# Key and value compression of a sparse-attention layer: block rows stationary, W1's rounded halves moving, a constant matrix that folds

## The chip, the cores and the metric

The kernel runs on one core of a Trainium2 chip. The metric is the device time of one execution in microseconds (us); the kernel before has a median of 1343.45 us over three runs (1343.28 to 1351.97). The engines are TensorE (PE; PEld is its weight load), VectorE (DVE), ScalarE (ACT), GpSimd (POOL) and SyncE (SP), whose queue issues most loads.

## The reference, cut to what matters

The program is two decoder layers over 512 tokens of width 1024. Each has a mixer (sparse attention, gated linear attention, spatial gating) and a gated feed-forward part. The change touches one step of the sparse attention, the compression of raw keys and raw values into 31 block rows for each of two groups:

```python
def compress_blocks(k_raw, pos_emb, w1, w2):
    B, S, G, hd = k_raw.shape                    # 1, 512, 2, 64
    nc = (S - CMP_LEN) // CMP_STRIDE + 1         # 31 blocks of 32 tokens, 16 apart
    idx = np.arange(nc)[:, None] * CMP_STRIDE + np.arange(CMP_LEN)[None, :]
    blk = k_raw[:, idx] + pos_emb[None, None, :, None, :]
    blk = blk.transpose(0, 1, 3, 2, 4).reshape(B, nc, G, CMP_LEN * hd)
    return jax.nn.gelu(blk @ w1) @ w2            # w1: 2048 x 256, w2: 256 x 64
```

It is called for keys (then rotated) and for values, in each layer. A block of 32 tokens is two runs of 16, and each run belongs to two blocks, as the first half of one and the second half of another.

## The kernel before, in words

Everything is float32 at the input. Large products are made from three f32r products: an operand is split into a rounded half (ScalarE, `nc.scalar.copy` to f32r) and the rest (VectorE, a subtraction), here called hi and lo. `w_rows` (lines 278 to 284) loads a 512 KB piece of a weight into a `raw` buffer (three of them) with a SyncE issue, and `w_split` (lines 266 to 276) splits it into an `hl` buffer (four of them). `mm3` (lines 285 to 288) issues hi x hi, hi x lo and lo x hi. The scheduler orders each engine's instructions when the program is built; each engine then runs its list in order, waiting on semaphores.

The stretch of the mixer that matters runs so. The projection for the spatial gating (`uv`) ends. `proj_feat` (lines 477 to 487) projects raw keys and raw values, features on partitions: two PSUM banks of 128 x 512, one for keys and one for values, with their matmuls taken in turn. `ev_kv` (lines 542 to 550) takes each bank out in four VectorE products with `rb`, the row of inverse norms, into `kvS`, 128 x 8 x 66: partitions are (token parity, feature), then a pair number within a run of 16 tokens, then the runs of both groups and two columns of the position embedding (`pos_t`).

Beside this `uv` is normalised: squares on ScalarE (line 560), a short chain on VectorE (lines 561 to 564), four scalings on VectorE (567), four additions on GpSimd (568). Then TensorE makes the four spatial products (571), VectorE gates them (574), and the result is transposed (444) and split.

The compression follows, first keys, then values (lines 580 to 647): W1 comes in eight 256 KB loads into buffers of its own (`w1` and `qr` tags), unsplit. It is the stationary operand, 128 x 128 at a time, and 65 columns of `kvS` move, all in f32; 16 steps of 128 rows times two halves of 256 hidden features, accumulated into one PSUM tile (line 593). The position columns give a bias (597), a Gelu follows (601), then W2. The keys' result is rotated, transposed and split (612 to 625), the values' is copied four times and split (632 to 645).

After that come the gates projection (`c1`, 296 columns, whose weights are three more `hl` units) and the `gqk` feature projection.

Of the kernel before, what the change touches and what calls it, by code (L numbers as in the profile page):

```python
# [19 lines left out]
P = 128  # L20
# [42 lines left out]
def shape_constants():  # L63
# [46 lines left out]
    for h in range(GH):  # L110
        hb[h * DK : (h + 1) * DK, h] = 1
        hones[h * DK : (h + 1) * DK, h] = 1
    triu = (j[:, None] <= i[None, :]).astype(np.float32)
    cf = np.concatenate([rope, ropec, hb.reshape(P, -1), triu, hones,
                         np.ones((P, 1), np.float32)], axis=1).astype(np.float32)
# [8 lines left out]
def trunk_kernel(ctx: ExitStack, tc: tile.TileContext, a, out):  # L124
# [10 lines left out]
    def nm(s):  # L135
        uid[0] += 1
        return f"{s}_{uid[0]}"
# [26 lines left out]
    hones = cf[:, o : o + GH]  # L164
    o += GH
    ones1 = cf[:, o : o + 1]
    mb = cp.tile([P, 2 * P + NT * 32], BF16, name="mb")
    identb = mb[:, 0:P]
    dmask = mb[:, P : 2 * P]
# [278 lines left out]
    def mixer(l, norm, xkt, eu=None):  # L448
# [8 lines left out]
        def xs(k, s):  # L457
            return xkt[k // 2][:, k % 2, s, :]
# [15 lines left out]
                with tc.high_priority(offset=EP.get(wsite[0], EPRI)):  # L474
                    evac(t, ps)

        def proj_feat(c0, evac):

            us = [w_rows(w_in, k0 * P, 4, c0, 256) for k0 in (0, 4)]
            ps = [psum("g") for _ in range(2)]  # L480
            for k in range(KT):
                for b in range(2):
                    u = us[k // 4][:, :, k % 4, b * P : (b + 1) * P]
                    mm3(ps[b], u[:, 0], u[:, 1], xs(k, 0), xs(k, 1), k == 0, k == KT - 1)
            for b in range(2):
                with tc.high_priority(offset=EP.get(wsite[0], EPRI)):
                    evac(b, ps[b])

        def units(c0, w, nks):
            us, k0 = [], 0  # L490
# [5 lines left out]
        with tc.tile_pool(name=f"mx{l}", bufs=1, reuse_waits="tile") as mp:  # L496
# [13 lines left out]
            with tc.tile_pool(name=f"ma{l}", bufs=1, reuse_waits="tile") as ap:  # L510
# [24 lines left out]
                nc.scalar.dma_start(lngb[:, 1, :], a["sg_ln_b"][l : l + 1, :].to_broadcast([P, 256]))  # L535
                rb = norm.broadcast()


                kvS = [ap.tile([P, 8, 66], F32, name=nm("kvS")) for _ in range(2)]
                for w_i in range(2):  # L540
                    nc.gpsimd.tensor_copy(kvS[w_i][:, :, 64:66], pos_t(w_i, l).rearrange("p (s a) -> p a s", s=2))

                def ev_kv(b, ps):
                    for g in range(G):
                        gs = slice(g * 64, (g + 1) * 64)
                        src = ps[gs, :].rearrange("p (c a r) -> p r a c", a=8, r=2)
                        rbv = rb[gs, :].rearrange("p (c a r) -> p r a c", a=8, r=2)
                        for lp in range(2):
                            nc.vector.tensor_tensor(kvS[b][lp * 64 : (lp + 1) * 64, :, g * 32 : (g + 1) * 32],
                                                    src[:, lp], rbv[:, lp], op=ALU.mult)  # L550
                site("kc")
                proj_feat(C_KC, ev_kv)

                vmean = small(NT, "vmean", 1)
                nc.vector.tensor_scalar(vmean, vsum, 1.0 / 256, None, op0=ALU.mult)
# [24 lines left out]
                hts = []  # L580
                for w_i, nmw in enumerate("kv"):
                    w1 = a["cmp_w1_" + nmw][l]
                    ps = psum("o")[:, 0:130]
                    for u in range(8):
                        if u % 5 < 3:
                            wu = ap.tile([P, 2, 256], F32, tag="w1", name=nm("w1"), bufs=6)
                        else:
                            wu = mp.tile([P, 2, 256], F32, tag="qr", name=nm("w1"), bufs=4)
                        nc.sync.dma_start(wu, w1[u * 256 : (u + 1) * 256, :].rearrange("(k p) c -> p k c", p=P))
# [6 lines left out]
                    hb = small(2, "hb", 2)  # L596
                    nc.scalar.copy(hb, ps.rearrange("p (k c) -> p k c", k=2)[:, :, 64])
                    hid = tmp(124)
                    hT = hid.rearrange("p (k c) -> p k c", k=2)
                    for hh in range(2):  # L600
                        nc.scalar.activation(hT[:, hh].rearrange("p (g c) -> p g c", g=G),
                                             ps[:, hh * 65 : hh * 65 + 64].rearrange("p (g c) -> p g c", g=G)[:, :, 0:NC_],
                                             AF.Gelu_apprx_tanh, bias=hb[:, hh : hh + 1])
# [811 lines left out]
```

## Time and profile before

| what | value |
|---|---|
| median of three runs | 1343.45 us |
| profiled execution | 1343.64 us, span 1341.9 us |
| TensorE busy | 1298.7 us, 97% |
| VectorE, ScalarE, GpSimd busy | 949.1, 624.5 and 176.4 us |
| chain that ended last, by engine | PE 77%, DVE 12%, ACT 4% |

Busy time is the union of an engine's instructions. Matmuls overlap, so a mean of a matmul is longer than the distance to the next start. Idle time stands in brackets behind a row, with what ended it.

### The profile page before, as it was taken

The page shows a single profiled execution, that of the slowest core. Times are in us where ns is not written, and L with a number is a line of the kernel's source. Part 1 is how long each engine was busy: PE and PEld are TensorE (multiplying, and loading weights), DVE is VectorE, ACT ScalarE, POOL GpSimd, SP SyncE. Part 2 cuts the span into 40 slices and gives each one's busy share as a digit, 9 for nine tenths or more (in the row PEclk, how much of TensorE's full clock was granted, in tenths as well). Part 3 has the DMA queues.
Part 4 walks back from the last instruction along what each step waited for, and adds up shares of the span by engine and source line. Part 5 has one row for each costly group of instructions (what it writes and reads, how often), then busy time and mean ns, then how long its engine had stood idle before and what let it go on. Part 6 is the DMA issues. An engine that isn't in the chain of part 4 may idle for free.

```text
span 1341.9 us, 17478 instructions
## 1 busy us (share of the span) xinstructions
PE 1298.7 (97%) x6434; PEld 1054.7 (79%) x6434; DVE 949.1 (71%) x1661; ACT 624.5 (47%) x1164; POOL 176.4 (13%) x158
## 2 busy tenths in 40 slices
PE   6999999999999999999999999999999999999997
PEld 5888776777888888888888877767788888888785
DVE  5636889997865785586644498999778457736775
ACT  6344336665542543254442632667544435514532
POOL 2111021114000100010312102111220001000103
PEclk9999999999999999999999999999999999999999
DMA  8521131006335785384363302201343348754721
GB/s 280 156 81 48 32 95 32 17 17 159 109 99 121 206 213 152 105 203 111 96 181 97 91 21 63 79 17 33 91 129 95 110 120 205 225 126 126 195 88 64
DMA packets 128554, 150.41 MB, mean 112 GB/s; under 512 B 9034, under 2 KB 82516, under 8 KB 128468
## 3 DMA queue, kind: packets, MB, share of 16 engines
q1 hardware_dynamic: 115504, 128.31, 31.5%
q0 software_dynamic: 8704, 16.78, 7.4%
q10 hardware_dynamic: 4260, 4.20, 1.1%
q8 instruction: 51, 0.84, 0.3%
q14 instruction: 35, 0.29, 0.1%
HBM read 147.17 MB, written 2.10 MB: 111 GB/s over the span
## 4 chain that ended last, share of the span: by engine, by line
PE 77%; DVE 12%; ACT 4%; DMA 3%; issue 3%; POOL 1%; SPq 0%; ACTq 0%; DVEq 0%; POOLq 0%
PE psg L286 10%; PE psg L287 10%; PE psg L288 10%; PE pss L286 4%; PE pst L286 4%; PE pss L288 4%; PE pss L287 4%; PE pst L288 4%; PE pst L287 4%; PE pso L593 2%; DVE hl L274 2%; PE pst L1010 2%; PE pso L288 2%; PE pso L286 2%; PE pso L287 2%
## 5 line engine op out<-in xcount | busy, mean ns | idle before, releaser
L271 ACT CAST hl<-raw 128x1024 fp32r<-128x1024 f32 (+3 forms) x170 | 175.6, 1034 | 224.3 <-PE pst L288 66.2
L274 DVE TENSOR_TENSOR hl<-raw,hl 128x1024 fp32r<-128x1024 f32 (+3 forms) x170 | 207.8, 1223 | 100.3 <-ACT hl L271 97.5
L286 PE MATMUL psg<-hl,kt 128*128 128x512 f32 (+2 forms) x480 | 179.4, 375 | 4.1 <-ACT hl L271 2.1
L288 PE MATMUL psg<-hl,kt 128*128 128x512 f32 (+2 forms) x480 | 178.2, 372 | 0.0
L287 PE MATMUL psg<-hl,kt 128*128 128x512 f32 (+2 forms) x480 | 177.3, 370 | 0.0
L286 PEld LDWEIGHTS psg<-hl,kt 128*128 128x128 f32 x480 | 91.1, 190 | 19.0 <-DVE gqk L698 2.7
L288 PEld LDWEIGHTS psg<-hl,kt 128*128 128x128 f32 x480 | 91.1, 190 | 12.9
L287 PEld LDWEIGHTS psg<-hl,kt 128*128 128x128 f32 x480 | 91.0, 189 | 12.8
L287 PE MATMUL psg<-kt,hl 128*128 128x512 f32 x248 | 99.6, 402 | 1.2 <-DVE kt L249 1.2
L286 PE MATMUL psg<-kt,hl 128*128 128x512 f32 x248 | 99.6, 403 | 0.0
L288 PE MATMUL psg<-kt,hl 128*128 128x512 f32 x248 | 98.3, 398 | 0.0
L271 ACT CAST hl<-wx 128x1024 fp32r<-128x1024 f32 x48 | 50.3, 1049 | 78.6 <-PE pst L288 63.3
L274 DVE TENSOR_TENSOR hl<-wx,hl 128x1024 fp32r<-128x1024 f32 x48 | 58.7, 1223 | 18.0 <-ACT hl L271 17.4
L253 ACT CAST PT<-pst 128x384 fp32r<-128x384 f32 (+1 forms) x96 | 46.7, 519 | 37.9 <-PE pst L1010 37.6
L254 DVE TENSOR_TENSOR PT<-pst,PT 128x384 fp32r<-128x384 f32 (+1 forms) x96 | 54.8, 595 | 10.5 <-ACT PT L253 9.6
L1002 POOL TENSOR_TENSOR P<-P,rr 128x512 f32<-128x512 f32 x32 | 35.5, 1109 | 174.8 <-DVE rr L999 134.3
L1010 PE MATMUL pst<-ident,P 128*128 128x128 f32 x320 | 53.2, 277 | 2.6 <-DVE P L1004 2.6
L287 PEld LDWEIGHTS psg<-kt,hl 128*128 128x128 f32 x248 | 46.9, 189 | 9.9 <-DVE kt L249 2.0
L288 PEld LDWEIGHTS psg<-kt,hl 128*128 128x128 f32 x248 | 46.8, 189 | 8.0
L286 PEld LDWEIGHTS psg<-kt,hl 128*128 128x128 f32 x248 | 46.7, 189 | 7.8 <-ACT kt L253 0.3
L286 PE MATMUL pss<-hl,kt 128*128 128x512 f32 x128 | 50.3, 393 | 1.7 <-DVE ft L1302 1.3
L288 PE MATMUL pss<-hl,kt 128*128 128x512 f32 x128 | 50.0, 390 | 0.0
(442 smaller groups left out, 3139.6 us busy)
## 6 DMA issues: line engine op xcount, KB each, us to landing
raw<-in_w_gate_dram SPq DMA_DIRECT2D x44, 512.0 KB, 3.8
raw<-in_w_up_dram SPq DMA_DIRECT2D x44, 512.0 KB, 4.4
raw<-in_w_in_dram SPq DMA_DIRECT2D x32, 512.0 KB, 3.7
raw<-in_w_down_dram SPq DMA_DIRECT2D x20, 512.0 KB, 3.9
raw<-in_w_down_dram SPq DMA_DIRECT2D x36, 256.0 KB, 4.1
raw<-in_w_out_dram SPq DMA_DIRECT2D x16, 512.0 KB, 4.0
w<-in_cmp_w_k_dram SPq DMA_DIRECT2D x16, 256.0 KB, 5.4
w<-in_cmp_w_v_dram SPq DMA_DIRECT2D x16, 256.0 KB, 3.1
```

The lines of the kernel that those rows point to most:

```text
L253: nc.scalar.copy(hi, src)
L254: nc.vector.tensor_tensor(lo, src, hi.bitcast(F32), op=ALU.subtract)
L271: nc.scalar.copy(hl[:, 0, 0:n], raw[:, 0:n])
L274: e_.tensor_tensor(hl[:, 1, 0:n], raw[:, 0:n], hl[:, 0, 0:n].bitcast(F32), op=ALU.subtract)
L286: nc.tensor.matmul(ps, lh, rh, start=start, stop=False, skip_group_check=skip)
L287: nc.tensor.matmul(ps, lh, rl, start=False, stop=False, skip_group_check=skip)
L288: nc.tensor.matmul(ps, ll, rh, start=False, stop=stop, skip_group_check=skip)
L593: nc.tensor.matmul(ps[:, hh * 65 : (hh + 1) * 65], wu[:, kk, hh * P : (hh + 1) * P], kvS[w_i][:, s % 8, s // 8 : s // 8 + 65], start=s == ...
L1002: nc.gpsimd.tensor_tensor(ps_[i], ps_[i], rr[:, i : i + 1].to_broadcast([P, P * (i + 1)]), op=ALU.mult)
L1010: nc.tensor.transpose(T[:, c : c + P], ps_[i][:, j * P : (j + 1) * P], ident)
```

## The change

Four things change in the mixer of each layer, and one constant is added.

First, `proj_feat` gets an argument `apart`: all 24 matmuls of the keys run before the 24 of the values, and the keys are taken out as soon as theirs are done. Second, the eviction copies PSUM to `kvS` on ScalarE (four copies each for keys and values), multiplies by `rbk` (a rearranged copy of `rb`) in one VectorE operation, and splits the result into `kvR`, in which hi and lo of a column lie side by side. The two position columns move to the ends of the 66 columns. Third, W1 is loaded by `w_rows` in four 512 KB pieces and split like other weights. The stationary operand is now 64 columns of `kvR` with both halves, 128 columns; W1's hi and lo move, 256 columns each. The first eight steps and the last eight accumulate in two halves of one PSUM tile. Fourth, the sums over hi and lo, over the two runs of a block and over the position row are made by a constant matrix `fold` (128 x 2 x 62, part of the constants' load): the PSUM tile is copied to SBUF, and four f32 matmuls per operand multiply it by `fold`. The Gelu then needs no bias.

The core of the diff:

```diff
+    fold = np.zeros((2, 64, 2 * NC_), np.float32)
+    r31 = np.arange(NC_)
+    fold[0, 0, :] = 1
+    fold[0, 1 + r31, r31] = 1
+    fold[0, 33 + r31, NC_ + r31] = 1
+    fold[1, r31, r31] = 1
+    fold[1, 32 + r31, NC_ + r31] = 1
+    fold[1, 63, :] = 1
+    fold = np.repeat(fold, 2, axis=1).transpose(1, 0, 2)
...
-        def proj_feat(c0, evac):
+        def proj_feat(c0, evac, apart=False):
...
+            for bs in ((0,), (1,)) if apart else ((0, 1),):
+                for k in range(KT):
+                    for b in bs:
+                        u = us[k // 4][:, :, k % 4, b * P : (b + 1) * P]
+                        mm3(ps[b], u[:, 0], u[:, 1], xs(k, 0), xs(k, 1), k == 0, k == KT - 1)
+                for b in bs:
+                    with tc.high_priority(offset=EP.get(wsite[0], EPRI)):
+                        evac(b, ps[b])
...
+                rbk = ap.tile([P, 8, 32], F32, name=nm("rbk"))
+                for lp in range(2):
+                    hs = slice(64 * lp, 64 * lp + 64)
+                    nc.scalar.copy(rbk[hs], rb[hs, :].rearrange("p (c a r) -> p r a c", a=8, r=2)[:, lp])
...
+                kvR = [ap.tile([P, 8, 66, 2], F32R, name=nm("kvR")) for _ in range(2)]
...
                         for lp in range(2):
-                            nc.vector.tensor_tensor(kvS[b][lp * 64 : (lp + 1) * 64, :, g * 32 : (g + 1) * 32],
-                                                    src[:, lp], rbv[:, lp], op=ALU.mult)
+                            nc.scalar.copy(kvS[b][lp * 64 : (lp + 1) * 64, :, 1 + g * 32 : 33 + g * 32], src[:, lp])
+                    k4 = kvS[b][:, :, 1:65].rearrange("p a (g c) -> p a g c", g=G)
+                    nc.vector.tensor_tensor(k4, k4, rbk.unsqueeze(2).to_broadcast([P, 8, G, 32]), op=ALU.mult)
+                    split_psum(kvR[b][:, :, :, 0], kvR[b][:, :, :, 1], kvS[b])
                 site("kc")
-                proj_feat(C_KC, ev_kv)
+                proj_feat(C_KC, ev_kv, True)
...
-                    ps = psum("o")[:, 0:130]
-                    for u in range(8):
...
-                        for kk in range(2):
-                            s = u * 2 + kk
-                            for hh in range(2):
-                                nc.tensor.matmul(ps[:, hh * 65 : (hh + 1) * 65], wu[:, kk, hh * P : (hh + 1) * P],
-                                                 kvS[w_i][:, s % 8, s // 8 : s // 8 + 65],
-                                                 start=s == 0 and hh == 0, stop=s == 15 and hh == 1, skip_group_check=True)
...
+                    ps = psum("o")
+                    for u in range(4):
+                        wu = w_rows(a["cmp_w1_" + nmw][l], u * 512, 4, 0, 256)
+                        for kk in range(4):
+                            s = u * 4 + kk
+                            s8 = s // 8
+                            for half in range(2):
+                                nc.tensor.matmul(ps[:, s8 * 256 : (s8 + 1) * 256], kvR[w_i][:, s % 8, 2 * s8 : 2 * s8 + 64, :].rearrange("p c h -> p (c h)"),
+                                                 wu[:, half, kk, :], start=s % 8 == 0 and half == 0, stop=s % 8 == 7 and half == 1,
+                                                 skip_group_check=True)
+                    hs_ = tmp()
+                    nc.scalar.copy(hs_, ps)
+                    hps = psum("s")
+                    for kk in range(2):
+                        for s8 in range(2):
+                            nc.tensor.matmul(hps[:, kk * 62 : kk * 62 + 62], hs_[:, s8 * 256 + kk * P : s8 * 256 + kk * P + P],
+                                             fold[:, s8, :], start=s8 == 0, stop=s8 == 1)
                     hid = tmp(124)
+                    nc.scalar.activation(hid, hps[:, 0:124], AF.Gelu_apprx_tanh)
```

How the change moves instructions is seen best on TensorE, from the spatial products of layer 0 to the keys' fold. Before, with `pso` the compression's PSUM tile, `kvS` the keys, `w` W1, `pss` the spatial products and `pst` the transposes of `uv`:

```order
L571 MATMUL pss_515<-uv_249,wsT_391 128x256
L571 MATMUL pss_518<-uv_249,wsT_391 128x256
L571 MATMUL pss_521<-uv_249,wsT_391 128x256
L593 MATMUL pso_542<-kvS_403,w_92_543 128x65 x4
L593 MATMUL pso_542<-kvS_403,w_93_549 128x65 x4
L593 MATMUL pso_542<-kvS_403,w_94_555 128x65 x4
L593 MATMUL pso_542<-kvS_403,w_95_561 128x65 x4
L593 MATMUL pso_542<-kvS_403,w_96_567 128x65
L571 MATMUL pss_524<-uv_249,wsT_391 128x256
L444 MATMUL pst_528<-ident,uv_249 128x128 x4
```

The same place in the changed program (lines 592, 456, 613 and 621 there are the spatial products, the transposes, W1 and the fold; `hl` is split W1, `kvR` the split keys):

```order
L592 MATMUL pss_528<-uv_249,wsT_391 128x256
L592 MATMUL pss_531<-uv_249,wsT_391 128x256
L592 MATMUL pss_534<-uv_249,wsT_391 128x256
L592 MATMUL pss_537<-uv_249,wsT_391 128x256
L456 MATMUL pst_541<-ident,uv_249 128x128 x4
L613 MATMUL pso_555<-hl_558,kvR_408 128x256 x8
L613 MATMUL pso_555<-hl_571,kvR_408 128x256 x8
L613 MATMUL pso_555<-hl_584,kvR_408 128x256 x6
L456 MATMUL pst_548<-ident,uv_249 128x128 x4
L613 MATMUL pso_555<-hl_584,kvR_408 128x256 x2
L613 MATMUL pso_555<-hl_597,kvR_408 128x256 x8
L621 MATMUL pss_610<-cf,tmp_608 128x62 x4
```

The fourth spatial product and the first transposes now stand ahead of W1, and the fold stands directly behind the keys' W1.

On ScalarE the place is the one after the last `uv` eviction (line 519 before, 532 after), up to the squares of `uv` (560 before, 581 after). Before (line 321 copies `rb`, 271 is the cast of a weight unit, here of the gates projection):

```order
L519 ACTIVATE uv_249<-pst_352,rstd_232 128x256
L321 COPY rb_401<-pst_396 128x512
L271 CAST hl_722<-raw_719 128x888
L560 ACTIVATE tmp_478,vssq_251<-uv_249 128x256
L560 ACTIVATE tmp_481,vssq_251<-uv_249 128x256
```

After (283 casts a unit of W1, 333 copies `rb`, 554 makes `rbk`, 568 takes the keys out, 265 rounds them):

```order
L532 ACTIVATE uv_249<-pst_352,rstd_232 128x256
L283 CAST hl_571<-raw_569 128x1024
L333 COPY rb_401<-pst_396 128x512
L581 ACTIVATE tmp_491,vssq_251<-uv_249 128x256
L554 COPY rbk_403<-rb_401 64x256 x2
L581 ACTIVATE tmp_494,vssq_251<-uv_249 128x256
L581 ACTIVATE tmp_497,vssq_251<-uv_249 128x256
L581 ACTIVATE tmp_500,vssq_251<-uv_249 128x256
L568 COPY kvS_406<-psg_424 64x8x32 x4
L265 CAST kvR_408<-kvS_406 128x528
L283 CAST hl_584<-raw_582 128x1024
```

The cast of a W1 unit moved ahead of `rb`, and two copies came in between the squares.

On SyncE the place is the issue of W1 behind the two units of the key and value projection. Before:

```order
L280 DMA raw_412<-in_w_in_dram 128x4x256
L589 DMA w_92_543<-in_cmp_w_k_dram 128x2x256
L589 DMA w_93_549<-in_cmp_w_k_dram 128x2x256
L589 DMA w_94_555<-in_cmp_w_k_dram 128x2x256
L589 DMA w_97_573<-in_cmp_w_k_dram 128x2x256
```

After:

```order
L292 DMA raw_419<-in_w_in_dram 128x4x256
L292 DMA raw_556<-in_cmp_w_k_dram 128x4x256
L292 DMA raw_569<-in_cmp_w_k_dram 128x4x256
L292 DMA raw_582<-in_cmp_w_k_dram 128x4x256
L292 DMA raw_595<-in_cmp_w_k_dram 128x4x256
L292 DMA raw_638<-in_cmp_w_v_dram 128x4x256
```

W1 now goes through the three `raw` buffers, and the gates projection's loads come behind all eight of its pieces.

## Rows read from the trace of the kernel before

**Rows 1.** The page, busy time of each engine

```profile
PE 1298.7 (97%) x6434; PEld 1054.7 (79%) x6434; DVE 949.1 (71%) x1661; ACT 624.5 (47%) x1164; POOL 176.4 (13%) x158
```

**Rows 2.** Windows: length, busy PE, PEld, DVE, ACT, POOL, PE clock, DMA share, GB/s

```profile
16.00:30.00 14.00, 14.00 (x66) 11.52 (x66) 9.72 (x14) 12.33 (x27) 6.00 (x8) 1.00 0.90 302
...
52.00:64.00 12.00, 10.10 (x81) 9.38 (x81) 8.31 (x15) 2.22 (x3) 0.72 (x2) 1.00 0.39 117
64.00:77.00 13.00, 13.00 (x107) 12.40 (x107) 2.09 (x12) 3.21 (x13) 1.46 (x3) 1.00 0.23 72
```

**Rows 3.** Timeline of PE, layer 0: start, length, instruction, [idle before, releaser]

```profile
51.73 0.39 PE L288 MATMUL psg<-kt,hl 128*128 128x512 f32 x1
52.31 1.56 PE L571 MATMUL pss<-uv,wsT 128*128 128x256 f32 x6 [0.19 <-POOL uv L568]
55.58 4.01 PE L593 MATMUL pso<-kvS,w 128*128 128x65 f32 x34 [1.70 <-DVE kvS L549]
...
67.83 5.13 PE L593 MATMUL pso<-kvS,w 128*128 128x65 f32 x44
72.77 0.39 PE L288 MATMUL psg<-hl,kt 128*128 128x296 f32 x1
...
86.91 0.39 PE L286 MATMUL psg<-kt,hl 128*128 128x512 f32 x1
```

**Rows 4.** Timeline of PE, layer 1, the same place

```profile
710.62 4.01 PE L593 MATMUL pso<-kvS,w 128*128 128x65 f32 x34 [1.72 <-DVE kvS L549]
```

**Rows 5.** Groups by form, PE, 36 to 112 us: busy us, mean ns, idle before

```profile
L593 PE MATMUL pso<-kvS,w 128*128 128x65 f32 x128 | 15.2, 275 | 1.7 <-DVE kvS L549 1.7
```

**Rows 6.** Timeline of PE: neighbouring starts at 512 and at 256 moving columns

```profile
45.16 0.39 PE L286 MATMUL psg<-kt,hl 128*128 128x512 f32 x1
45.39 0.39 PE L287 MATMUL psg<-kt,hl 128*128 128x512 f32 x1
...
101.40 0.28 PE L286 MATMUL psg<-hl,kt 128*128 128x256 f32 x1
101.52 0.28 PE L287 MATMUL psg<-hl,kt 128*128 128x256 f32 x1
```

**Rows 7.** Groups by form, DVE, 30 to 112 us

```profile
L274 DVE TENSOR_TENSOR hl<-raw,hl 128x1024 fp32r<-128x1024 f32 x8 | 9.8, 1224 | 11.3 <-ACT hl L271 11.1
...
L254 DVE TENSOR_TENSOR ghl<-tmp,ghl 128x512 fp32r<-128x512 f32 x1 | 0.7, 693 | 0.8 <-ACT ghl L253 0.8
```

**Rows 8.** Groups by form, ACT, 30 to 112 us

```profile
L271 ACT CAST hl<-raw 128x1024 fp32r<-128x1024 f32 x9 | 9.4, 1047 | 7.4 <-PE psg L288 6.7 <-PE pst L288 0.7
...
L658 ACT ACTIVATE gv<-psg,rstd 128x256 f32<-128x256 f32 x4 | 1.9, 467 | 0.0
...
L253 ACT CAST ghl<-tmp 128x512 fp32r<-128x512 f32 x1 | 0.6, 620 | 0.8 <-DVE tmp L690 0.8
```

**Rows 9.** DMA issues, KB each, us to landing: page, then 10 to 110 us

```profile
raw<-in_w_in_dram SPq DMA_DIRECT2D x32, 512.0 KB, 3.7
...
w<-in_cmp_w_k_dram SPq DMA_DIRECT2D x8, 256.0 KB, 7.9
```

**Rows 10.** Timeline of SP: the first issue into the buffer freed at 38.5 us

```profile
38.51 0.37 SPq L670 DMA_DIRECT2D raw<-in_w_in_dram  x1
```

**Rows 11.** Timeline of ACT: the copy of rb

```profile
41.93 0.59 ACT L321 COPY rb<-pst 128x512 f32<-128x512 f32 x1 [0.74 <-PE pst L319]
```

**Rows 12.** Timeline of DVE: from the squares' sums to the scalings

```profile
45.19 0.17 DVE L562 TENSOR_SCALAR vvar<-vssq 128x4 f32<-128x4 f32 x1 [0.52 <-ACT tmp L560]
...
47.65 0.48 DVE L567 SCALAR_TENSOR_TENSOR uv<-uv,vr,lngb 128x256 f32<-128x256 f32 x1
48.05 0.77 DVE L274 TENSOR_TENSOR hl<-raw,hl 128x592 fp32r<-128x592 f32 x1
48.74 2.23 DVE L567 SCALAR_TENSOR_TENSOR uv<-uv,vr,lngb 128x256 f32<-128x256 f32 x3
```

**Rows 13.** Line 567 from 47 to 53 us: duration ns least, median, most

```profile
L567 DVE SCALAR_TENSOR_TENSOR uv<-uv,vr,lngb x4: 472/720/961, 47.6 to 50.0; 128x256 f32<-128x256 f32 x4
```

More of the change, by code (lines that the diff above doesn't have):

```diff
@@ L113, in shape_constants @@
     triu = (j[:, None] <= i[None, :]).astype(np.float32)
+    fold = np.zeros((2, 64, 2 * NC_), np.float32)
[7 more added lines that the diff above has]
+    fold = np.repeat(fold, 2, axis=1).transpose(1, 0, 2)
     cf = np.concatenate([rope, ropec, hb.reshape(P, -1), triu, hones,
-                         np.ones((P, 1), np.float32)], axis=1).astype(np.float32)
+                         np.ones((P, 1), np.float32), fold.reshape(P, -1)], axis=1).astype(np.float32)
     return {"eye": np.eye(P, dtype=np.float32), "cf": cf, "tsel": tsel.reshape(P, -1), "cm": np.concatenate([masks8, mb], axis=1).astype(np.float32)}
@@ L166, in trunk_kernel @@
     ones1 = cf[:, o : o + 1]
+    o += 1
+    fold = cf[:, o : o + 4 * NC_].rearrange("p (s c) -> p s c", s=2)
     mb = cp.tile([P, 2 * P + NT * 32], BF16, name="mb")
@@ L475, in proj_tok @@
                     evac(t, ps)
-        def proj_feat(c0, evac):
+        def proj_feat(c0, evac, apart=False):
             us = [w_rows(w_in, k0 * P, 4, c0, 256) for k0 in (0, 4)]
             ps = [psum("g") for _ in range(2)]
[L481 to L487, printed above, removed]
+            for bs in ((0,), (1,)) if apart else ((0, 1),):
[6 more added lines that the diff above has]
+                        evac(b, ps[b])
         def units(c0, w, nks):
@@ L536, in mixer @@
                 rb = norm.broadcast()
+                rbk = ap.tile([P, 8, 32], F32, name=nm("rbk"))
+                for lp in range(2):
+                    hs = slice(64 * lp, 64 * lp + 64)
+                    nc.scalar.copy(rbk[hs], rb[hs, :].rearrange("p (c a r) -> p r a c", a=8, r=2)[:, lp])
                 kvS = [ap.tile([P, 8, 66], F32, name=nm("kvS")) for _ in range(2)]
+                kvR = [ap.tile([P, 8, 66, 2], F32R, name=nm("kvR")) for _ in range(2)]
                 for w_i in range(2):
-                    nc.gpsimd.tensor_copy(kvS[w_i][:, :, 64:66], pos_t(w_i, l).rearrange("p (s a) -> p a s", s=2))
+                    pa = pos_t(w_i, l).rearrange("p (s a) -> p a s", s=2)
+                    nc.gpsimd.tensor_copy(kvS[w_i][:, :, 0:1], pa[:, :, 0:1])
+                    nc.gpsimd.tensor_copy(kvS[w_i][:, :, 65:66], pa[:, :, 1:2])
                 def ev_kv(b, ps):
                     for g in range(G):
-                        gs = slice(g * 64, (g + 1) * 64)
-                        src = ps[gs, :].rearrange("p (c a r) -> p r a c", a=8, r=2)
-                        rbv = rb[gs, :].rearrange("p (c a r) -> p r a c", a=8, r=2)
+                        src = ps[g * 64 : (g + 1) * 64, :].rearrange("p (c a r) -> p r a c", a=8, r=2)
                         for lp in range(2):
-                            nc.vector.tensor_tensor(kvS[b][lp * 64 : (lp + 1) * 64, :, g * 32 : (g + 1) * 32],
-                                                    src[:, lp], rbv[:, lp], op=ALU.mult)
+                            nc.scalar.copy(kvS[b][lp * 64 : (lp + 1) * 64, :, 1 + g * 32 : 33 + g * 32], src[:, lp])
+                    k4 = kvS[b][:, :, 1:65].rearrange("p a (g c) -> p a g c", g=G)
+                    nc.vector.tensor_tensor(k4, k4, rbk.unsqueeze(2).to_broadcast([P, 8, G, 32]), op=ALU.mult)
+                    split_psum(kvR[b][:, :, :, 0], kvR[b][:, :, :, 1], kvS[b])
                 site("kc")
-                proj_feat(C_KC, ev_kv)
+                proj_feat(C_KC, ev_kv, True)
                 vmean = small(NT, "vmean", 1)
@@ L596, in mixer @@
-                    hb = small(2, "hb", 2)
-                    nc.scalar.copy(hb, ps.rearrange("p (k c) -> p k c", k=2)[:, :, 64])
+                    site("w1")
+                    ps = psum("o")
[8 more added lines that the diff above has]
+                                                 skip_group_check=True)
@@ L599, in mixer @@
                     hT = hid.rearrange("p (k c) -> p k c", k=2)
[L600 to L603, printed above, removed]
                     w2 = ap.tile([P, 2, HD], F32, tag="w2", name=nm("w2"), bufs=2)
```

5 lines of the change are left out of this document (removed).

## The prediction

> **What bounds the kernel now.** I read the page's busy line first [rows 1]: TensorE is busy 97% of the span, VectorE 71%. Time can be saved only where TensorE has less to do or waits less, and added work on VectorE or ScalarE costs only where it makes TensorE wait. The order of the two programs differs only around the key and value compression, once per layer, so I read that stretch. The table by stage shows 10.1 of 12 us busy from 52 to 64 us, all of 13 us from 64 to 77 us, and the clock at its full level (2.4 GHz) in both [rows 2]. In TensorE's timeline [rows 3] the stretch runs from the last matmul of the key and value projection (51.73 us, ends 52.1) to the first one of the next feature projection (86.91 us): 34.8 us. In it lie a wait of 0.19 us for GpSimd's last addition to `uv`, a wait of 1.70 us for VectorE's eviction of `kvS` (eight instructions after the projection), and the compression matmuls of line 593. Layer 1 repeats it, 655.04 us later [rows 4]. All sums below are for one layer and count twice.
>
> **The change, part by part.**
>
> *W1's matmuls.* Line 593 leaves 128 records per layer [rows 5]. The row's mean of 275 ns is pipelined, so the pace is taken from starts: 44 records from 67.83 to 72.77 us [rows 3], 0.112 us each. Removed: 128 x 0.112 = 14.3 us. Now 64 matmuls move 256 columns against 128 stationary ones. The same form in the `gr` projection starts every 0.12 us [rows 6]: added 64 x 0.120 = 7.7 us.
>
> *The fold.* Eight matmuls of 62 moving columns per layer. They are f32, as line 593's are, so each should be two records at 0.112 us: added 1.8 us. Together TensorE's work changes by -14.3 + 7.7 + 1.8 = -4.8 us.
>
> The rows say that a record of 65 columns takes far longer than its columns: 512 take 0.227 us and 256 take 0.12 [rows 6], so 65 would take 0.03, and 0.112 is what is seen. The Trainium skill ("TensorE: Matmul & The Clock Gate", section "Back-to-back issue gap") gives a matmul by itself N/2.4 + 2.5 ns. By that rule alone W1 would cost some 3.8 us before and 7.0 us after, and the change would add TensorE work; the same section says that a stream with weight loads is set by both. The rows of this kernel side with the second remark, and the sum goes by the rows.
>
> *Eviction of keys ahead of values.* The keys' half of the projection ends some 5.6 us earlier than the values' half (24 matmuls at 0.227 us). Four ScalarE copies, one product, one rounding and one subtraction for the keys then run beside the values' matmuls. Their chain is about 4 x 0.47 + 0.69 + 0.62 + 0.69 = 3.9 us with nothing in front, by the nearest rows [rows 7, 8]. The values' chain is hidden behind W1 for the keys (32 x 0.12 = 3.8 us, and the spatial products and transposes before it). The wait of 1.70 us goes: -1.7 us. If this cover were gone, up to 3.9 us would come back.
>
> *What is late next: the spatial products.* They follow the projection on TensorE and need `uv` normalised. On ScalarE the second W1 unit's cast now stands ahead of the copy of `rb`. Its raw buffer comes free at 38.5 us (the next issue into it shows that [rows 10]) and a 512 KB load lands in 3.7 us [rows 9], so the cast runs 42.3 to 43.3, `rb` to 43.9; two new half-height copies of `rb` (0.4 us each from start to start, a little under a 128x256 one [rows 8]) stand among the four squares. Before, `rb` was copied at 41.93 us [rows 11] and VectorE had the last square at 45.19 [rows 12]; now that comes near 46.6 us: +1.4 us. On VectorE the 2.46 us chain from there to the first scaling [rows 12] shifts by as much. Between the scalings the subtraction of 592 columns goes (0.69 us, from 48.05 to 48.74) and the keys' product and subtraction come (0.69 each): +0.7 us. These also stand beside GpSimd's additions; the four scalings show what that costs, 0.47 us alone and up to 0.96 beside them [rows 13]. Before, TensorE reached the products just 0.19 us ahead of GpSimd, so the lateness shows in full: +2.1 us. Bounds: 0.5 (the load lands earlier, the copies hide) to 4 (all three new VectorE operations at double time).
>
> *The copy before the fold.* TensorE must wait for a ScalarE copy of the 128x512 result (0.59 us, as `rb`'s eviction [rows 11]) and two hand-overs: 0.8 us for the keys. The values' copy has the gates projection's first matmuls beside it: zero, at most 0.8. Together +0.8.
>
> *Rounding W1.* Per layer eight units more, each a ScalarE cast of 1.05 us and a VectorE subtraction of 1.22 us [rows 7, 8]; the page's VectorE total should rise by about 2 x 8 x 1.22 = 20 us. Two units are rounded under the projection, when VectorE has room. The other six take 7.3 us; the three units of the gates projection, moved behind them, 2.8 by their columns; four gatings 1.8; the values' product and subtraction and two output roundings 2.7; the keys' rotation and the copies for the values 1.7: some 16.5 us of VectorE work after 53.4 us, when the normalising ends there. It can end at 69.9 us; I take 71.7, because a unit also waits for a raw buffer. There are three, each turn costing 3.7 us of load and 2.3 us of rounding. TensorE's own work to the end of the first gates tile ends near 72.8 us (18 us of matmuls from 54.2, and the fold's wait). Cover and work end nearly together, so I set this at zero, with up to 2.5 us against. On SyncE's queue eight 512 KB loads stand where sixteen of 256 KB stood, and the gates loads come behind all of them; later loads, issued against the same buffers, come no later than their use needs. The larger constant load (124 columns more) lands long before the fold. GpSimd's four copies of position rows instead of two are done before the projection starts: nothing.
>
> *Sum.* -4.8 - 1.7 + 2.1 + 0.8 = -3.6 us per layer, -7.2 us in all. The profiled execution took 1343.64 us (span 1341.9), 0.19 above the median of the runs, 1343.45. Forecast: **1336.4 us**, between 1333.5 and 1340 when only the sizes above are off. I give it 0.60.
>
> **The rivals.**
>
> *Everything is covered (0.12).* Lateness at the spatial products and the fold's wait are filled or absent: -4.8 - 1.7 + 0.5 = -6 us per layer, 1331.6. For it: before, VectorE is busy 2.1 of the 13 us from 64 to 77 us [rows 2]. Against: the six hand-overs ahead of the spatial products are in order on two engines.
>
> *The weight pipeline gives most of it back (0.21).* The last gates unit comes 2 to 3.5 us later than I take it: -1.6 to 0 us per layer, 1340.4 to 1343.6. For it: three raw buffers, no prefetch of W1 into buffers of its own any more. Against: VectorE's 16.5 us fit.
>
> *The raw buffers make it slower (0.05).* Place: the two turns of one buffer between the second values' unit and the last gates unit. The forecast leaves 3.6 us, so it decides when a 512 KB load takes 1.8 us more per turn, 5.5 us instead of 3.7. At 7.9 us, which the W1 loads of the keys show in a busy stretch [rows 9], two turns cost 8.4 us: +4.8 us per layer, 1353. Against: that stretch had 0.9 of the DMA engines busy, and this one has 0.39 and 0.23 [rows 2].
>
> *The matmuls don't get cheaper (0.02).* If a record cost its moving columns, 0.443 ns each by the 512-column rows, W1 would go from 128 x 0.029 = 3.7 to 64 x 0.113 = 7.3 us, and the fold add 0.4: +4.0 - 1.7 + 2.9 = +5.2 per layer, 1354. Line 593's 0.112 us speaks plainly against it. It is the case in which the Trainium skill's formula for a single matmul (the section named above) would hold here.
>
> A fall of the granted clock in the new waits is not in these: the wait of 1.70 us shows none [rows 2, 3].
>
> **How the numbers follow.** The time is the forecast's, 1336.4. The forecast's own spread, the covered case and the weight pipeline's case hold over nine tenths; the range of 8 in 10 reaches from the covered case to near the old time: 1331.5 to 1342.5. About 1%, 13.4 us, is what can be told from no change. Faster by more would need 6.7 us per layer, above the covered case: 0.03. Slower by more needs more than the last two rivals reach at their prices: 0.02. Within 1%: 0.95.
>
> **What would show it.** In the profile after, the W1 matmuls should start every 0.12 us and number 128, the 32 fold records every 0.11; the wait before W1 for `kvS` should be gone and one of about 2 us stand before the spatial products, put down to GpSimd or VectorE; a wait of about 0.8 us for the copy before the keys' fold; from the projection's end to the next feature projection 31.2 us instead of 34.8. The prediction is wrong if TensorE waits for `hl` by more than 2.5 us per layer in the W1 or gates matmuls, or if the time moves elsewhere than in these two stretches.

## The result, and the profile after

The changed kernel takes 1338.93 us (median of 14 runs, 1335.15 to 1344.17) against 1348.11 us for the kernel before in the same comparison (14 runs): ratio 0.9939, 95% interval 0.9924 to 0.9955. The forecast was 1336.4, range 1331.5 to 1342.5. The number held. The way to it did not, and most of this part is about that. The forecast was counted from 1343.45 us, below the median that before has here, so it was 7.2 us of gain that were forecast and 9.2 that were measured.

The profiled execution took 1340.79 us, span 1339.0. Its busy line on the page answers to [rows 1]: VectorE has 14.9 us more, ScalarE 27, TensorE 9.9 us less.

```profile
PE 1288.8 (96%) x6338; PEld 1049.9 (78%) x6338; DVE 964.0 (72%) x1669; ACT 651.7 (49%) x1200; POOL 179.1 (13%) x162
```

TensorE's timeline in layer 0 answers to [rows 3] (start, length, instruction, idle time before it and its releaser). Line 592 is the spatial products, 456 the transposes, 613 W1, 621 the fold.

```profile
52.30 0.39 PE L300 MATMUL psg<-kt,hl 128*128 128x512 f32 x1
56.17 3.47 PE L592 MATMUL pss<-uv,wsT 128*128 128x256 f32 x8 [3.49 <-POOL uv L589]
59.44 0.85 PE L456 MATMUL pst<-ident,uv 128*128 128x128 f32 x4
60.04 2.86 PE L613 MATMUL pso<-hl,kvR 128*128 128x256 f32 x22
62.73 0.60 PE L456 MATMUL pst<-ident,uv 128*128 128x128 f32 x4
...
65.21 1.10 PE L621 MATMUL pss<-cf,tmp 128*128 128x62 f32 x8 [0.68 <-ACT tmp L617]
66.12 0.96 PE L613 MATMUL pso<-hl,kvR 128*128 128x256 f32 x6
...
72.05 0.41 PE L299 MATMUL psg<-hl,kt 128*128 128x296 f32 x1 [0.58 <-DVE hl L286]
...
87.27 0.39 PE L298 MATMUL psg<-kt,hl 128*128 128x512 f32 x1
```

From the start of the projection's last matmul to the start of the next feature projection it is 34.97 us; before it was 35.18 [rows 3]. (The prediction counts from that matmul's end, which makes both 0.39 us shorter; this part counts from its start.) So the stretch in which everything was meant to happen gained 0.2 us per layer, not 3.6. The cheap matmuls are there: 22 W1 records in 2.69 us are 0.122 us each, eight fold records in 0.91 us are 0.114 each. But TensorE waits 3.49 us for the spatial products, and then the eight records of line 592 take 3.27 us to the next start, 0.41 each. Layer 1 repeats it:

```profile
708.07 3.43 PE L592 MATMUL pss<-uv,wsT 128*128 128x256 f32 x8 [3.59 <-POOL uv L589]
711.29 0.89 PE L456 MATMUL pst<-ident,uv 128*128 128x128 f32 x4
```

The windows (busy time by engine, then the granted clock, the DMA share and GB/s) answer to [rows 2]. The clock was 1.00 in both before; now it is 0.86 in the first, so part of it ran at 1.2 GHz.

```profile
52.00:64.00 12.00, 8.51 (x49) 7.26 (x48) 9.29 (x13) 7.16 (x11) 3.69 (x3) 0.86 0.29 89
64.00:77.00 13.00, 11.74 (x91) 10.89 (x90) 9.30 (x20) 7.78 (x14) 2.04 (x4) 1.00 0.76 205
```

Where, then, do the microseconds come from? Laying equal matmuls of the two traces side by side, the lead of the changed kernel grows by 3.1 us in layer 0's feed-forward part and by 3.8 us in layer 1's, whose code is untouched. TensorE's windows of 30 us there (busy time and count, clock, DMA share, GB/s) show it. First before, then after:

```profile
636.00:666.00 30.00, 30.00 (x130) 1.00 0.34 97
```

```profile
636.00:666.00 30.00, 30.00 (x134) 1.00 0.37 106
```

Both are full, at full clock, with no wait, and after fits in four matmuls more: a 512-column matmul starts every 0.2267 us, before every 0.2333. That pace is the larger half of the result: 6.5 us, added up below.

In these two profiles 4.1 us of the lead are lost again between 1270 and 1300 us, in the middle of layer 1's. TensorE waits there for VectorE's `ft`, whose chain goes back to weight loads, 3.30 us instead of 1.29, and twelve matmuls behind the wait start every 0.43 us instead of 0.23: the clock fell there too. Before, then after:

```profile
1273.47 0.50 PE L286 MATMUL pss<-hl,kt 128*128 128x512 f32 x1 [1.29 <-DVE ft L1302]
```

```profile
1269.42 0.79 PE L298 MATMUL pss<-hl,kt 128*128 128x512 f32 x1 [3.30 <-DVE ft L1324]
...
1270.44 0.63 PE L300 MATMUL pss<-hl,kt 128*128 128x512 f32 x1
1270.87 0.63 PE L298 MATMUL pss<-hl,kt 128*128 128x512 f32 x1
```

The same kernel's profile in e1 has the wait (2.90 us) without the fall, and loses 1.1 us.

### The profile page after: what moved, and what is told of

Its sections match the earlier page's. It is cut to its first block, busy times and chain, and to the rows that moved or that the text cites. A ratio compares the mean times of both kernels' runs of the same rounds, so it can differ in the third digit from the quotient of the medians.

```text
span 1339.0 us, 17347 instructions
## 1 busy us (share of the span) xinstructions
PE 1288.8 (96%) x6338; PEld 1049.9 (78%) x6338; DVE 964.0 (72%) x1669; ACT 651.7 (49%) x1200; POOL 179.1 (13%) x162
## 4 chain that ended last, share of the span: by engine, by line
PE 72%; DVE 13%; ACT 6%; DMA 4%; issue 3%; POOL 1%; SPq 0%; ACTq 0%; DVEq 0%; POOLq 0%
PE psg L299 9%; PE psg L298 9%; PE psg L300 9%; PE pss L298 4%; PE pss L299 4%; PE pss L300 4%; PE pst L298 4%; PE pst L300 4%; PE pst L299 4%; DVE hl L286 2%; PE pso L298 2%; PE pso L299 2%; PE pso L300 2%; ACT hl L283 2%; PE pst L1032 2%
## 5 line engine op out<-in xcount | busy, mean ns | idle before, releaser
L286 DVE TENSOR_TENSOR hl<-raw,hl 128x1024 fp32r<-128x1024 f32 (+3 forms) x186 | 227.0, 1223 | 107.1 <-ACT hl L283 105.0
L283 ACT CAST hl<-raw 128x1024 fp32r<-128x1024 f32 (+3 forms) x186 | 192.3, 1036 | 214.7 <-PE pst L300 64.8
L1024 POOL TENSOR_TENSOR P<-P,rr 128x512 f32<-128x512 f32 x32 | 35.4, 1107 | 174.5 <-DVE rr L1021 126.0
L299 PE MATMUL pss<-hl,kt 128*128 128x512 f32 x128 | 50.8, 397 | 0.0
```

The source lines that it names most:

```text
L283: nc.scalar.copy(hl[:, 0, 0:n], raw[:, 0:n])
L286: e_.tensor_tensor(hl[:, 1, 0:n], raw[:, 0:n], hl[:, 0, 0:n].bitcast(F32), op=ALU.subtract)
L1024: nc.gpsimd.tensor_tensor(ps_[i], ps_[i], rr[:, i : i + 1].to_broadcast([P, P * (i + 1)]), op=ALU.mult)
```

## The experiments

### Is it the program, and is it the larger constants?

e1 is the changed kernel unedited.

> The changed kernel once more, beside the kernel before. Theory A (the compression stretch gives the gain): from the projection's last matmul to the next feature projection it must be about 3 us per layer shorter than before's 35.2 us. Theory B (the stretch gives almost nothing, since a wait of 3.5 us and half clock behind it eat what the matmuls save; the gain comes from matmuls outside it, whose pace is a property of the program): the stretch is again 35.0 us, the wait before the spatial products again 3.5 us in both layers, the feed-forward's 512-column matmuls again start every 0.2267 us, and the time is again 0.6% below before. Theory C (pace outside the stretch is chance of a run): the stretch as in B, but the feed-forward's pace lies anywhere between 0.2267 and 0.2334 us, and the ratio nearer to 1.

Measured: 1337.78 us, ratio 0.9939 [0.9922, 0.9957]; stretches 34.7 and 35.2 us, waits 3.51 and 3.57 us, feed-forward pace 0.2267 throughout. Theory B holds, A and C fall.

e2 edits the kernel before:

```diff
-                         np.ones((P, 1), np.float32)], axis=1)
+                         np.ones((P, 1), np.float32), fold.reshape(P, -1)], axis=1)
```

> The kernel before with only the constant array made larger by the 496 bytes per partition of the fold matrices; nothing reads them. It moves what is placed behind it in SBUF and adds 64 KB to one load. If the gain outside the stretch comes from where tiles lie, this kernel gains about 6 to 8 us like the changed one (ratio 0.994 to 0.996) and its feed-forward pace is 0.2267 us throughout. If it comes from the instruction stream (fewer matmul records, other order) or from chance of a run, the ratio is 1.000 within 0.0015.

Measured: 1347.48 us, ratio 1.0006 [0.998, 1.0031], slow pace as in before. I took that as a finding against place in SBUF. It was not, for a reason seen only afterwards: it moves everything behind it by the same 512 bytes.

### What the wait before the spatial products costs

e3 and e4 edit the changed kernel; e3 takes the keys' lead back, e4 moves the normalising of `uv` ahead of `rbk` and the projection:

```diff
-                proj_feat(C_KC, ev_kv, True)
+                proj_feat(C_KC, ev_kv)
```

```diff
                 rb = norm.broadcast()
+                vmean = small(NT, "vmean", 1)
+                ...
+                    nc.gpsimd.tensor_tensor(v, v, lngb[:, 1, :], op=ALU.add)
                 rbk = ap.tile([P, 8, 32], F32, name=nm("rbk"))
```

> The changed kernel with the projection's two halves interleaved again, as before; W1's rounded halves and the fold stay. In the order of instructions the keys' product and subtraction no longer stand between VectorE's four scalings, but a W1 subtraction does (1.2 us in place of 1.9), so the wait before the spatial products should be about 2.8 instead of 3.5 us. In return all eight eviction copies start after the projection, and W1's first matmul is held until about 59 us by kvR. If keys-ahead matters as the change says, the stretch grows from 35.0 to 36 or 37 us (time 2 to 4 us above the changed kernel's). If the spatial products' wait is all that counts, it shrinks to about 34.3 us (1 to 1.5 us below the changed kernel).

Measured: 1338.45 us, ratio 0.9942 [0.9922, 0.9961], no different from e1; stretches 36.0 and 35.4 us. The stretch of layer 0 grew as the first case had it, the time did not, so neither case came out. The wait before the products is 2.43 us, but W1 now waits too:

```profile
55.17 1.99 PE L592 MATMUL pss<-uv,wsT 128*128 128x256 f32 x8 [2.43 <-POOL uv L589]
57.01 0.60 PE L456 MATMUL pst<-ident,uv 128*128 128x128 f32 x4
59.84 2.72 PE L613 MATMUL pso<-hl,kvR 128*128 128x256 f32 x13 [2.23 <-DVE kvR L266]
```

Taking the keys out first is worth what it hides, 1.3 to 2.2 us of W1's wait, of which the longer wait for the products gives most back.

> The changed kernel with the normalising of uv written ahead of the keys' copies of rb and the projection: on ScalarE the four squares now come ahead of the two copies of rb, on VectorE three scalings come ahead of the keys' product and all four ahead of its subtraction. Theory B1 (the wait of 3.5 us, and the half clock behind it, hold back what the matmuls save): squares end 1.3 us earlier (46.2 instead of 47.6), the last addition on GpSimd near 53 instead of 56.1, wait before the spatial products 0.5 us or less, no fall of the granted clock there; the stretch becomes 31 to 32 us per layer and the time 6 to 8 us below the changed kernel's (about 1331). Theory B2 (the W1 units from VectorE are what ends last anyway, the wait is only moved): the wait reappears before W1 or the gates matmuls and the stretch stays within 1 us of 35.0.

Measured: 1329.29 us, ratio 0.9875 [0.9855, 0.9895], 8.5 us below e1, the best of the kernels with e8 (below, no different). The stretches are 31.0 and 31.5 us.

```profile
53.24 2.18 PE L592 MATMUL pss<-uv,wsT 128*128 128x256 f32 x8 [1.11 <-POOL uv L565]
55.25 0.60 PE L456 MATMUL pst<-ident,uv 128*128 128x128 f32 x4
55.60 2.86 PE L613 MATMUL pso<-hl,kvR 128*128 128x256 f32 x22
```

The clock stays at full speed there (1.00 behind the engines' busy times):

```profile
48.00:58.00 10.00, 8.89 (x51) 7.32 (x50) 9.80 (x15) 6.76 (x12) 4.07 (x4) 1.00 0.20 56
```

In layer 0 the wait is 2.4 us shorter, and products and first transposes take 2.36 us to W1's first matmul instead of 3.87: 1.5 us less at full clock. Together 3.9 of the 3.95 us by which the stretch is shorter. B1 is shown, though 1.11 us of the wait were left, not 0.5: the keys' product, still ahead of the fourth scaling, took 1.23 us beside GpSimd.

### What sets the pace of matmuls nobody touched

The diff removes `hb`, a small tile with two buffers of 32 bytes. All tiles allocated behind it move 64 bytes against those ahead of it (`hl`, `kt`). The feed-forward multiplies `hl` and `kt` with `act` and `op7`, which lie behind. In the built programs `hl` starts at byte 39456 of each partition and `act` at 141920 before, at 39968 and 142368 after. e5 edits before, e6 the changed kernel; neither changes an instruction.

```diff
-                    hb = small(2, "hb", 2)
+                    hb = small(2, "hb", 4)
```

```diff
-                vvar = small(NT, "vvar", 1)
+                vvar = small(NT, "vvar", 2)
...
-                vr = small(NT, "vr", 1)
+                vr = small(NT, "vr", 2)
```

> The kernel before with one number changed: the small tile hb gets four buffers instead of two. No instruction differs; every tile placed behind hb in SBUF moves by 64 bytes, so that the feed-forward's act and op7 start at 32 instead of 96 bytes past a multiple of 128, which is where the changed kernel has them (it drops hb). Theory P (place in SBUF sets the pace of the 512-column matmuls; 0.2333 us with a stationary operand at 96, 0.2267 at 32): the feed-forward's pace is 0.2267 us throughout, and the time falls by 6 to 8 us, ratio 0.994 to 0.9955, without any change to the compression. Theory I (the instruction stream, of which the changed kernel has fewer TensorE records, sets it): no change, ratio 1.000 within 0.0015.

Measured: 1352.4 us, ratio 1.0027 [0.9995, 1.006]; pace still 0.233. Theory P, as I had put it, is wrong: 32 past a multiple of 128 is not what matters.

> The changed kernel with the small tiles vvar and vr given two buffers instead of one: 64 bytes more ahead of the large tiles, no instruction differs, act and op7 are at 96 again as in before. Theory P: its feed-forward slows to 0.2333 us, the time rises by 6 to 8 us over the changed kernel's, ratio to before 0.999 to 1.001: what the compression's new form is worth by itself, with its two stretches of 35.0 us against 35.2. Theory I: no change, ratio 0.994.

Measured: 1345.01 us, ratio 0.9969 [0.9947, 0.9991]. With not one instruction changed, 64 bytes cost 7.2 us against e1 by the medians, and each of e6's twelve runs is longer than each of e1's six. By the two ratios, each to its own runs of before, it is 4.0 us. The window in its feed-forward reads as before's:

```profile
636.00:666.00 30.00, 30.00 (x130) 1.00 0.36 103
```

In the profiles e6 falls behind e1 by 3.1 us between 395 and 675 us and by 5.0 us from 1050 us to the end, and by 0.4 us in all the rest. In the 5.0 are 1.7 us of a clock fall behind e6's wait for `ft`, which e1 has not, less 0.8 us of shorter waits. Beside before, where `act` and `op7` lie at the same places within 256 bytes, e6's lead changes by less than 0.4 us through either feed-forward part up to that wait.

e7, e8 and e10 add zeros behind e4's constants (24, 8 and 16 columns), so that all large tiles move together; e9 and e11 move `act` and `op7` alone, in before and in e4:

```diff
-fold.reshape(P, -1)], axis=1)
+fold.reshape(P, -1), np.zeros((P, 24), np.float32)], axis=1)
```

```diff
-                    hb = small(2, "hb", 2)
+                    hb = small(64, "hb", 2)[:, 0:2]
```

```diff
-                vr = small(NT, "vr", 1)
+                vr = small(68, "vr", 1)[:, 0:NT]
```

> The kernel with the statistics first, and 96 bytes of zeros more in the constant array, which nothing reads: hl, kt, act, op7 and nearly all other large tiles start at a multiple of 128 bytes instead of 32 past one. If the pace depends on how many pieces of 64 or 128 bytes an operand's row touches, a multiple of 128 is the best place: the 512-column pace falls below 0.2267 us (by as much as it rose from 32 to 96, 0.0067 us, that is to 0.220: about 20 to 25 us for the program, near 1306). If 32 is as good as 0, the pace stays 0.2267 us and the time stays within 2 us of 1329.

> As the run before, with 32 bytes of zeros more instead of 96: the large tiles start at 64 past a multiple of 128. If only the half of 128 bytes counts in which a row starts, the pace is that of 96, 0.2333 us, and the program is 20 to 30 us longer than 1329. If the place within 64 bytes counts, it is the same as at 0. If 32 and 64 are as good as each other, 1329.

> The kernel before with the small tile hb (two columns used) made 64 columns wide, twice 256 bytes: no instruction differs, all tiles behind hb move by 448 bytes, so that the feed-forward's act and op7 start at the same place within 512 bytes (32) as hl and kt. The runs so far leave two rules: R (relative: a 512-column matmul takes 0.2267 us where its two operands start at the same place within 512 bytes, and 0.2304 to 0.2334 us where they are 64 or 128 bytes apart) and A (absolute: 0, 32, 64 and 128 within 512 are good, 96 and 160 are not). Both expect here what 64 bytes alone did not bring: pace 0.2267 us throughout, and 6 to 8 us less, ratio 0.994 to 0.996, without any change to the compression. If neither holds, 1.000.

> The kernel with the statistics first, and 64 bytes of zeros more in the constant array: hl, kt, act and op7 all start at 96 within 512 bytes. Rule R: operands are 0 apart, pace 0.2267 us, time as with 0, 32 and 64: 1329 within 1.5. Rule A: 96 is a bad place, all 512-column matmuls slow, 0.2333 us: 20 us or more longer.

> The kernel with the statistics first and the small tile vr made 256 bytes wider: hl and kt stay at 32 within 512 bytes, act and op7 go to 288, so that they are 256 bytes apart. Rule R: the matmuls with act or op7 slow to 0.230 to 0.2335 us, 5 to 9 us longer than 1329. If only distances of 64 and 128 hurt (a cycle of 256 bytes or less), 1329. Rule A says nothing of 288.

The paces, from starts of three matmuls in a row without a wait (some 700 with `act` or `op7` stationary, 500 with `act` moving, 2500 with `hl` and `kt` alone, which take 0.227 in every kernel). "Apart" is the distance of the start of `act` from that of `hl`, modulo 256 bytes:

| kernel | `hl` mod 256 | apart | `act`, `op7` stationary | `act` moving | time, us |
|---|---|---|---|---|---|
| before | 32 | 64 | 0.2333 | 0.2304 | 1348 |
| e2 | 32 | 64 | 0.2333 | 0.2290 | 1347.5 |
| e5 | 32 | 128 | 0.2328 | 0.2334 | 1352.4 |
| e9 | 32 | 0 | 0.2267 | 0.2269 | 1342.9 |
| changed | 32 | 0 | 0.2267 | 0.2269 | 1338.9 |
| e6 | 32 | 64 | 0.2333 | 0.2304 | 1345.0 |
| e4 | 32 | 0 | 0.2267 | 0.2269 | 1329.3 |
| e7, e8, e10 | 128, 64, 96 | 0 | 0.2267 | 0.2269 | 1330.1, 1328.7, 1330.3 |
| e11 | 32 | 0 (256) | 0.2267 | 0.2269 | 1329.9 |

Rule R holds as far as it was tried, but with a cycle of 256 bytes, not 512: at 256 apart e11 is not slow. Distances other than 0, 64, 128 and 256 were not tried. Rule A falls with e10. The faster pace that e7 hoped for and the slow one of e8's first case did not come. Added up from start to start in the profiles, the matmuls with `act` or `op7` are 6.5 us longer in e6 than in e1, and 6.5 us shorter in e9 than in before. And e9 is before with the right 448 bytes: no compression changed, ratio 0.9961 [0.993, 0.9991], its feed-forward 2.5 and 3.5 us faster than before's in the profiles, with 134 matmuls in the window from 636 to 666 us.

e9 shows a second thing. Its profiled run took 1353.13 us, because of this, in layer 1 (windows as above, all engines; then TensorE's timeline):

```profile
700.00:710.00 10.00, 8.10 (x44) 6.47 (x44) 9.31 (x15) 1.05 (x1) 4.10 (x5) 1.00 0.21 57
710.00:720.00 10.00, 10.00 (x51) 9.71 (x50) 2.84 (x6) 1.17 (x2) 0.00 (x0) 0.54 0.46 137
720.00:745.00 25.00, 25.00 (x113) 24.36 (x113) 2.09 (x12) 3.30 (x13) 1.46 (x3) 0.50 0.17 53
```

```profile
707.98 5.03 PE L593 MATMUL pso<-kvS,w 128*128 128x65 f32 x34 [1.74 <-DVE kvS L549]
```

After the same wait for `kvS` that cost nothing more in [rows 4], the clock fell to 1.2 GHz and stayed there through the 65-column matmuls and the gates projection: the stretch took 50.8 us. Of the four profiles with before's instructions two have such a fall (e5 lost 3.3 us to it); of those with the new compression none stays at 1.2 GHz for more than a few us here. Before's runs, one of 4877.74 us aside, spread over 1342 to 1363 us, with mean granted clocks of 0.999 to 0.985 where they were recorded; the changed kernel's over 1335 to 1344, with 0.992 to 0.996. That could explain e6: by its runs it is 0.3% faster than before, while its profile is 1.8 us longer than the undisturbed one of before, by what happens from its wait for `ft` on. The clocks on record point the same way. In e6's comparison the five runs of before with a granted clock of 0.998 or more took 1343.2 to 1345.6 us, the eighteen others 1345.5 to 1362.1, and e6's twelve 1342.8 to 1348.3. Beside those five the new compression at the old pace shows no gain. What brings the fall, and whether it is all of this rest, no run here settles.

### GpSimd beside VectorE

e12 edits e4; besides moving the additions to VectorE it puts them and the scalings ahead of the rest in the order:

```diff
+                with tc.high_priority(offset=EPRI):
                 ...
-                    nc.gpsimd.tensor_tensor(v, v, lngb[:, 1, :], op=ALU.add)
+                    nc.vector.tensor_tensor(v, v, lngb[:, 1, :], op=ALU.add)
```

> The kernel with the statistics first, and GpSimd's four additions to uv given to VectorE, with the scalings, ahead of the keys' product. Theory: VectorE and GpSimd slow each other when both work on SBUF (the subtraction of 592 columns took 1.23 us beside an addition on GpSimd and 0.71 alone; GpSimd's additions take 1.1 to 1.6 us). On VectorE alone four scalings and four additions take 8 x 0.4 = 3.2 us and end near 51.4, before the projection's end at 52.1: the wait of 1.1 us before the spatial products goes, 1 us per layer less, near 1327. Rival: the two engines do not hinder each other and the additions are now in series: end near 52.5 to 53, no gain, or the keys' subtraction comes late and W1 waits 0.5 to 1 us: 1329 to 1331.

Measured: 1329.8 us, ratio 0.986 [0.9815, 0.9906], no different from e4. (The subtraction of 1.23 us that the expectation names has 528 columns, not 592.) In VectorE's timeline eight operations run from 46.82 to 49.76 us, 0.37 us a piece, and TensorE comes to the products without a wait:

```profile
46.82 0.88 DVE L565 SCALAR_TENSOR_TENSOR uv<-uv,vr,lngb 128x256 f32<-128x256 f32 x2
47.62 0.75 DVE L566 TENSOR_TENSOR uv<-uv,lngb 128x256 f32<-128x256 f32 x2
48.29 0.87 DVE L565 SCALAR_TENSOR_TENSOR uv<-uv,vr,lngb 128x256 f32<-128x256 f32 x2
49.08 0.75 DVE L566 TENSOR_TENSOR uv<-uv,lngb 128x256 f32<-128x256 f32 x2
49.76 0.68 DVE L586 TENSOR_TENSOR kvS<-kvS,rbk 128x512 f32<-128x512 f32 x1
```

The stretches are 30.8 and 30.9 us, 0.3 to 0.6 less than e4's: of the wait of 1.11, others (0.62 us inside the products, and 0.50 for `hl` where e4 had 0.26) took most back in layer 0, and what is left is below the spread of the runs. The theory's mechanism is there, its gain is not.

## Why the prediction was right or wrong, step by step

**W1, fold and the `kvS` wait** came as forecast: 0.122 us for 0.120, 0.114 for 0.112, 64 and 16 records per layer, no wait before W1. The rows of this kernel, not the formula for a lone matmul, gave the price. (24 matmuls at 0.227 us are 5.4 us, not the 5.6 of the keys' lead; nothing hung on it.)

**The fold's copy** costs 0.68 us (0.8 forecast). **Rounding W1**: TensorE waits 0.58 and 0.49 us for `hl`, inside the 0 to 2.5 given. VectorE's total rose by 14.9 us, not 20: the forecast counted W1's subtractions alone, not what the eviction loses and gains there.

**The spatial products' lateness was mis-sized**: a wait of 3.49 us where there was one of 0.19, 3.3 us for the 2.1 forecast (inside the bounds of 0.5 to 4). ScalarE's rows show the smaller part: the two copies of `rb` take 0.64 us each, not 0.4.

```profile
43.08 1.05 ACT L283 CAST hl<-raw 128x1024 fp32r<-128x1024 f32 x1 [1.32 <-DMA raw<-in_cmp_w_k_dram]
...
44.92 1.28 ACT L554 COPY rbk<-rb 64x256 f32<-64x256 f32 x2
...
47.04 0.40 ACT L581 ACTIVATE tmp<-uv 128x256 f32<-128x256 f32 x1
```

The cast of W1 starts at 43.08, not 42.3, but that is no part of it. This profile as a whole lies 0.57 us behind the one of before by then (the projection's last matmul starts at 52.30, not 51.73), and in e1's profile, with the same wait, the cast starts on the forecast:

```profile
42.33 1.05 ACT L283 CAST hl<-raw 128x1024 fp32r<-128x1024 f32 x1 [1.35 <-DMA raw<-in_cmp_w_k_dram]
```

So VectorE has the last square at 47.57 us where [rows 12] had 45.19: with the 0.57 us off, 1.8 us late, not 1.4. From the first scaling to TensorE's products it is 6.2 us where it was 4.7, 1.5 us more for the 0.7 forecast; VectorE's and GpSimd's rows show that part:

```profile
47.57 0.17 DVE L583 TENSOR_SCALAR vvar<-vssq 128x4 f32<-128x4 f32 x1 [2.18 <-ACT tmp L581]
...
50.01 0.48 DVE L588 SCALAR_TENSOR_TENSOR uv<-uv,vr,lngb 128x256 f32<-128x256 f32 x1
50.42 0.69 DVE L570 TENSOR_TENSOR kvS<-kvS,rbk 128x512 f32<-128x512 f32 x1
51.02 1.36 DVE L588 SCALAR_TENSOR_TENSOR uv<-uv,vr,lngb 128x256 f32<-128x256 f32 x2
52.30 1.23 DVE L266 TENSOR_TENSOR kvR<-kvS,kvR 128x528 fp32r<-128x528 f32 x1
53.46 0.94 DVE L588 SCALAR_TENSOR_TENSOR uv<-uv,vr,lngb 128x256 f32<-128x256 f32 x1
...
60.50 0.71 DVE L266 TENSOR_TENSOR kvR<-kvS,kvR 128x528 fp32r<-128x528 f32 x1
```

```profile
50.58 1.12 POOL L589 TENSOR_TENSOR uv<-uv,lngb 128x256 f32<-128x256 f32 x1 [22.07 <-DVE uv L588]
52.06 2.06 POOL L589 TENSOR_TENSOR uv<-uv,lngb 128x256 f32<-128x256 f32 x2 [0.36 <-DVE uv L588]
54.48 1.64 POOL L589 TENSOR_TENSOR uv<-uv,lngb 128x256 f32<-128x256 f32 x1 [0.36 <-DVE uv L588]
```

The keys' subtraction, begun behind an addition on GpSimd, takes 1.23 us, and the values' one 0.71 alone; the keys' product, begun 0.16 us ahead of an addition, takes 0.69. The Trainium skill ("SBUF — State Buffer", section "Who interferes with whom") has the two engines share a pair of ports under an exclusive lock, which a VectorE operation with two SBUF inputs takes part in; these rows agree, in that the later of two is the longer one, but they show no lock.

**The clock was ruled out, wrongly.** "A fall of the granted clock in the new waits is not in these: the wait of 1.70 us shows none [rows 2, 3]." The new wait was twice that one, and behind it 0.41 us per record instead of 0.25 cost 1.5 us per layer (e4 gives it back). The Trainium skill ("TensorE: Matmul & The Clock Gate", section "HAM oscillation — how this bites in real kernels") tells of bursts that start at half clock after a wait; the trace agrees. And e9 shows that even the old wait, in another execution, had such a fall behind it: one profile without it was no bound.

**The sum of the stretch**: from the projection's end, as the prediction counts it, 34.6 us, not 31.2. The 3.4 us are 1.2 (lateness), 1.5 (clock), 0.6 (`hl`) and 0.2 of small pieces, less 0.1 (the fold's copy). With statistics first the stretch, counted so, is 30.6 and 31.1: the gain forecast was real, and lay behind that wait.

**The step that failed is the first one**: "The order of the two programs differs only around the key and value compression, once per layer, so I read that stretch." Equal order was taken for equal time. The feed-forward's instructions are the same, but two buffers of 32 bytes fewer put `act` and `op7` at the same place within 256 bytes as `hl`, and some 1200 matmuls became 1.5 to 3% cheaper: 6.5 us from start to start, 7.2 by the medians of e6 and e1. No rival named this either. The forecast named what would prove it wrong, "if the time moves elsewhere than in these two stretches"; it did. That the number held is luck: by chance about as much came from there as was missing in the two stretches, 3.4 us in each.

## What to carry to other kernels

Before reading where a change acts, compare the pace of matmuls that it did not touch: a tile dropped or resized moves everything allocated behind it, and here 64 bytes were worth 7.2 us, what the whole change was forecast to bring. Make the starts of both operands of the long matmul streams equal modulo 256 bytes, which a pad on a small tile does. Where a change adds work to an engine that ends a short chain (squares, statistics, scalings), write the chain first, and count a wait on TensorE with the clock behind it.

## What the runs showed of the hardware that was not expected

Of these streams a 512-column f32r matmul takes 0.2267 us where its operands start at equal places modulo 256 bytes, and 0.229 to 0.2334 us where they are 64 or 128 bytes apart; where both lie does not matter (32, 64, 96 and 128 modulo 256 measured alike). The Trainium skill ("SBUF — State Buffer", section "Who interferes with whom") calls TensorE's two read ports, for the moving operand and for weights, independent; by that the distance should not matter, and the measurement decides. What in the memory does it was not measured.

In e9 a wait of 1.74 us was followed by 1.2 GHz from near 711 until near 745 us while TensorE was busy with 65-column f32 matmuls and the gates projection; the same place in the profile before shows 1.70 to 1.72 us and full clock.
